# Moving the overflow branch behind the seventh quad's first products, the routing weights ahead, and the scaled residual off TensorE, in a two-layer decoder kernel

## The chip, the cores and the metric

The kernel runs on one core of a Trainium2 chip. The metric is the device time of one execution in microseconds: the median of the runs shown. All tensors are float32.

## What is computed

256 tokens of width 1024 pass two layers. Each has a mixer (layer 0: a gated MLP beside latent attention; layer 1: sparse attention in three branches), and behind it a mixture of 32 experts in 4 groups of 8. Each sub-layer ends in `x <- LN(alpha*x + f(x))`:

```python
for layer in range(DEPTH):
    ...
    x = layer_norm(DN_ALPHA * x + mix, ln1_g[layer], ln1_b[layer])
    ffn = hier_moe(x, ...)
    x = layer_norm(DN_ALPHA * x + ffn, ln2_g[layer], ln2_b[layer])
```

`hier_moe` picks one group per token by softmax, then two of its eight experts, and sums `silu(x w_gate) * (x w_up) * weight` times `w_down` over the chosen experts. The weights of all experts are 96 MB per layer; all are read.

## The kernel before, in words

**Weights.** Every weight matrix comes from memory as a piece of 1 MB into one of 23 places in SBUF (`Ring`, L106 to L140). `ring.free` gives a place back and at once records the load of the next piece in it, on SyncE's queue (SP). SP issues in order. At most eight loads are under way: each takes the semaphore of the eighth before it, so in a busy stretch SP issues one when one has landed.

**End of a mixer.** `project` (L448) forms `alpha*x + y w_o` in four PSUM banks `acc[t][h]` (token half t, column half h). The first matmul on each is `aident` (the identity times alpha) by `x`; then come eight steps of three matmuls each on operands that were split in a high and a low part by ScalarE (ACT) and VectorE (DVE). `close_mixer` (L476) copies the sums to `x` by ACT and takes their moments by DVE (`raw`, L481), transposes them, forms the router's logits, and picks groups and experts on DVE (`route`, L1227; `rank`, L1268; `places`, L1352, a 0/1 matrix of slots by tokens). Idle stretches of TensorE (PE) are filled with matmuls that nobody reads (`warm`, L335).

**Experts.** The 32 experts are taken as eight quads (`QUADS` gives the order); a quad works on 128 slots, 32 tokens for each of its four experts, or on two such chunks for quads 6 and 7 of layer 1 (`STATIC_CHUNKS`). A quad has twelve pieces: eight for gate and up (`gate_up`, L1417), four for down (`down`, L1454). `quad(i)` (L1490) forms the gate and up products of its tokens, gathers the tokens of the next quad (`pick`, L1367), prepares the way back (`back`, L1390), turns the hidden values, multiplies by down, and leaves the scatter into the sums `acc` for the next quad's gate and up products (`flush`). In the first quad three things are still missing and are recorded behind its gate and up products: the routing weights (`weights0`, `weights1` in `rest`, L549), `back` of the first quad, and `alpha*x` in the sums (four `aident` matmuls, L1524).

**Overflow.** Should an expert have over 32 tokens (64 in a quad of two chunks), `overflow` (L1292) does the rest in loops under a branch (`tc.If`, L1299) that every engine takes: each loads a count into a register, compares, and jumps over the body when it is zero. It stands between quads 5 and 6 (`OVERFLOW_AT = 6`, L1567 to L1575). With these inputs the body isn't entered.

The order of instructions on an engine is the order in which the code records them inside `manual_schedule`; the mixers and the first steps of `project` (`AUTO`) are ordered by a scheduler.

Of the kernel before, what the change touches and what calls it, by code (L numbers as in the profile page):

```python
# [142 lines left out]
def trunk(ctx, tc, a, out):  # L143
# [109 lines left out]
    aident = consts.tile([128, 128], F32, name="aident")  # L253
    idb = consts.tile([128, 128], BF16, name="idb")
    zerob = consts.tile([128, 128], BF16, name="zerob")
# [11 lines left out]
    def more_constants():  # L267
# [4 lines left out]
        V.memset(zerob, 0.0)  # L272
        V.tensor_scalar(aident, ident, ALPHA, None, op0=ALU.mult)
# [174 lines left out]
    def project(l):  # L448
# [27 lines left out]
    def close_mixer(l, rb, acc, step, products):  # L476
# [50 lines left out]
        for h in range(2):  # L527
            mm(acc2[0][h], zerob, idb[:, None, :].to_broadcast([128, 4, 128]), True, False)
        warm(2)
# [5 lines left out]
        for h in range(2):  # L535
            mm(acc2[1][h], zerob, idb[:, None, :].to_broadcast([128, 4, 128]), True, False)
        warm(W1[0])
# [16 lines left out]
        return rt, acc2, (xg, [second] + affines, rest)  # L554
# [737 lines left out]
    def overflow(l, rt, acc):  # L1292
# [6 lines left out]
        with tc.If(value(8, 56) > 0):  # L1299
# [7 lines left out]
    def more(l, q, g, acc):  # L1307
# [8 lines left out]
        p = ps("C")  # L1316
# [73 lines left out]
    def back(q, rt, dd, tr, often=True):  # L1390

        d, dw = dd[:, 0:256], (p2() if dd.shape[1] == 256 else dd[:, 256:512])[:, 0:256]
        V.tensor_tensor(dw.rearrange("p (t e s) -> p t e s", t=2, e=4), d.rearrange("p (t e s) -> p t e s", t=2, e=4),
                        rt[1][:, :, 4 * q:4 * q + 4, None].to_broadcast([128, 2, 4, 32]), op=ALU.mult)
        p = ps(tr)
# [13 lines left out]
    def gather(q, rt, base, tr):  # L1409
# [5 lines left out]
        return xg, *back(q, rt, dd, tr, often)  # L1415

    def gate_up(l, q, xgs, between):  # L1417

        hp = [ps("CO"[i]) for i in range(len(xgs))]
        for k in range(KC):  # L1420
# [6 lines left out]
            ring.free((l, q, k))  # L1427
# [50 lines left out]
    def moe_layer(l, rt, acc, begun):  # L1478
# [3 lines left out]
        gs, late = [(begun[0], None, None)], begun[1:]  # L1482
# [7 lines left out]
        def quad(i):  # L1490
# [4 lines left out]

            def between(k):
# [196 lines left out]
```

## Time and profile before

| | |
|---|---|
| median of 3 runs | 700.41 us (700.06 to 701.95) |
| the profiled execution's own time | 700.38 us |
| its span, first to last instruction | 698.7 us |
| PE busy | 619.1 us, 89% |
| DVE busy | 284.3 us, 41% |
| ACT busy | 204.5 us, 29% |
| DMA, mean over the span | 337 GB/s |
| mean granted clock of PE | 0.956 of full speed |

The span is cut in stretches, and for each the profile tells how long every engine was busy, which share of its full clock PE was granted, and how busy the 16 DMA engines were. In a stretch with PE idle the row of what it waited for says why. A stretch with PE never idle is limited by PE's own work, one with the DMA engines at a share of 1 is moving weights as fast as it can, and both can hold at once.

### The profile page before, as it was taken

Reading aid. Unit: us, or ns where it says so; the run is one execution under the profiler, and the core shown is the slowest. Engines: PE = TensorE matmul, PEld = TensorE weight load, DVE = VectorE, ACT = ScalarE, POOL = GpSimd, SP = SyncE. Lnnn points to the kernel's source line nnn. Section 1 sums busy time; section 2 is a strip of 40 time slices with the busy share of each in tenths; the row PEclk is TensorE's granted clock in tenths of the full one; section 3 lists DMA queues with packets and bytes.
Section 4 is the critical chain, followed back from the end, with each engine's and each line's share of the span. In section 5 each row is a group of like instructions: output and inputs, shape, how many; then the busy total and the mean of one; then the engine's idle time right before and its main releaser. Section 6 shows DMA issues by size and latency. Waiting matters only on the chain. (4 is left out here: it accounts for less than half of the span.)

```text
span 698.7 us, 11137 instructions
## 1 busy us (share of the span) xinstructions
PE 619.1 (89%) x4459; PEld 386.7 (55%) x4459; DVE 284.3 (41%) x709; ACT 204.5 (29%) x514; POOL 49.6 (7%) x56
## 2 busy tenths in 40 slices
PE   7799999799999685887999999999799899897883
PEld 5678676464555141423988776685554554644331
DVE  4757736522222120206848897444422212312116
ACT  5554534121111010103546676431111111202011
POOL 4611000000000000002420000000000000000002
PEclk9999999989999988997999999999899999999797
DMA  8946879949999999999498450399689999999961
GB/s 344 418 184 247 334 264 380 398 189 425 419 420 418 423 420 416 421 420 416 161 422 342 127 235 1 129 394 401 280 353 420 420 422 421 420 419 422 414 266 60
DMA packets 34068, 235.62 MB, mean 337 GB/s; under 512 B 3920, under 2 KB 4688, under 8 KB 6224
## 3 DMA queue, kind: packets, MB, share of 16 engines
q1 hardware_dynamic: 34000, 234.75, 82.7%
q8 instruction: 38, 0.62, 0.4%
q14 instruction: 30, 0.25, 0.1%
HBM read 233.69 MB, written 1.05 MB: 336 GB/s over the span
## 5 line engine op out<-in xcount | busy, mean ns | idle before, releaser
L182 PE MATMUL psC<-ring,w 128*32 128x512 f32 (+1 forms) x1040 | 132.5, 618 | 24.5 <-PEq L1299 13.1
L182 PEld LDWEIGHTS psC<-ring,w 128*32 128x32 f32 (+1 forms) x1040 | 31.2, 114 | 90.0 <-issue 48.5
L182 PE MATMUL psA<-ring,ring 128*128 128x256 f32 (+1 forms) x480 | 80.1, 315 | 0.0
L182 PE MATMUL psT<-ring,p 128*32 128x512 f32 (+1 forms) x608 | 68.8, 587 | 3.1 <-DMA ring<-in_moe 2.2
L182 PEld LDWEIGHTS psA<-ring,ring 128*128 128x128 f32 x480 | 67.5, 193 | 6.5 <-issue 1.8
L182 PEld LDWEIGHTS psT<-p,x 128*128 128x128 f32 x512 | 64.5, 208 | 10.9 <-issue 10.1
L182 PE MATMUL psT<-p,x 128*128 128x128 f32 x512 | 67.3, 295 | 0.0
L1437 DVE SCALAR_TENSOR_TENSOR p<-p,psC 128x256 f32<-128x256 f32 x16 | 6.7, 421 | 133.5 <-ACT p L1436 133.3
L317 DVE TENSOR_TENSOR p<-psT,p 128x256 fp32r<-128x256 f32 x72 | 30.5, 424 | 62.8 <-ACT p L316 62.8
L1436 ACT ACTIVATE p<-psC 128x256 f32<-128x256 f32 x16 | 6.1, 383 | 170.2 <-PE psC L182 170.2
L316 ACT ACTIVATE p<-psT 128x256 fp32r<-128x256 f32 x72 | 27.5, 383 | 63.2 <-PE psT L182 42.2
L290 POOL TENSOR_TENSOR sm<-sm,mhalf 128x1 f32<-128x1 f32 (+1 forms) x12 | 7.7, 647 | 511.4 <-DVE sm L287 280.6
L182 PEld LDWEIGHTS psA<-p,k 128*128 128x128 f32 x144 | 25.2, 192 | 30.1 <-issue 17.6
L182 PE MATMUL psA<-p,k 128*128 128x256 f32 x144 | 39.4, 313 | 1.6 <-DVE sm L1560 1.6
L312 DVE TENSOR_TENSOR ring<-ring,ring 128x1024 fp32r<-128x1024 f32 (+1 forms) x28 | 36.0, 1301 | 8.0 <-ACT ring L311 7.7
L182 PEld LDWEIGHTS psT<-ring,p 128*32 128x32 f32 x608 | 17.3, 111 | 37.6 <-issue 25.3
L182 PE MATMUL psS<-ring,ring 128*128 128x416 f32 (+3 forms) x128 | 32.0, 384 | 2.0 <-ACT ring L311 1.5
L182 PE MATMUL psO<-ring,ring 128*64 128x256 f32 (+3 forms) x248 | 32.2, 349 | 1.1 <-DVE ring L333 0.7
L311 ACT ACTIVATE ring<-ring 128x1024 fp32r<-128x1024 f32 (+1 forms) x32 | 31.8, 1031 | 3.6 <-issue 1.3
L182 PE MATMUL psS<-p,k 128*128 128x256 f32 x144 | 29.9, 288 | 0.0
L1377 DVE COPY w<-psT 128x512 f32<-128x512 f32 x16 | 11.1, 691 | 44.2 <-PE psT L182 44.2
L1111 ACT ACTIVATE ring<-psS,sm 128x128 f32<-128x128 f32 (+1 forms) x64 | 26.2, 420 | 7.8 <-DVE sm L1102 7.7
(282 smaller groups left out, 844.4 us busy)
## 6 DMA issues: line engine op xcount, KB each, us to landing
ring<-in_moe SPq DMA_DIRECT2D x192, 1024.0 KB, 19.5
ring<-in_m SPq DMA_DIRECT2D x23, 1024.0 KB, 10.0
ring<-in_vec SPq DMA_DIRECT2D x2, 1024.0 KB, 18.1
ring<-in_m SPq DMA_DIRECT2D x2, 832.0 KB, 6.0
x<-in_x SPq DMA_DIRECT2D x2, 512.0 KB, 5.2
out<-x SPq DMA_DIRECT2D x4, 256.0 KB, 2.0
ring<-in_m SPq DMA_DIRECT2D x1, 768.0 KB, 15.0
ring<-in_m SPq DMA_DIRECT2D x1, 736.0 KB, 18.9
```

The costliest lines, as they stand in the source:

```text
L182: T.matmul(o, lhsT, rhs, start=start, stop=stop, skip_group_check=True)
L290: G.tensor_tensor(r, t, mhalf[:, :n], op=ALU.pow)
L311: S.activation(hi, src, AF.Copy)
L312: (sub or V).tensor_tensor(lo, src, hi.bitcast(F32), op=ALU.subtract)
L316: S.activation(hi, src, AF.Copy)
L317: V.tensor_tensor(lo, src, hi.bitcast(F32), op=ALU.subtract)
L1111: S.activation(p[:, i * w:(i + 1) * w], sx[c, u][:, i * w:(i + 1) * w], AF.Exp, bias=nb[:, i0 + i:i0 + i + 1], accum_out=su[:, i0 + i:i0 + ...
L1377: (S.activation(dst, p[0], AF.Copy) if f == 0 else V.tensor_copy(dst, p[0]))
L1436: S.activation(e, p[:, 0:256], AF.Tanh, scale=0.5)
L1437: V.scalar_tensor_tensor(e, e, 1.0, p[:, 0:256], op0=ALU.add, op1=ALU.mult)
```

## The change

- The overflow branch moves from in front of quad 6 to behind that quad's gate and up products. `quad` becomes a generator that stops there (`yield`). The eight places of these products are given back, and the slots of the next quad formed, only behind the branch. PE gets a branch hint, recorded just before those products, with the label of the branch. In the body the bank "C" gives way to "O".
- The routing weights (`weights0`, `weights1`, and the weighted one-hot matrix of the first quad, now `weighted`) are recorded behind the first of the eight gate and up steps of the first quad. For the other quads `weighted` is recorded together with `places`, ahead of `back`.
- `alpha*x` gets into the experts' sums by four ACT instructions that write PSUM (`residual`), in place of four `aident` matmuls. In `project` the four `aident` matmuls go as well: `raw` forms `alpha*x + acc` by one DVE instruction per half, and takes the moments from the result in SBUF.
- The zero matmuls that opened the sums become matmuls of `warm`, in the same number. `router_prep(1)` moves from quad 3 to quad 5 of layer 0. The scratch space for DMA descriptors grows from 512 to 1024 bytes per partition.

```diff
         def products(t, i):
             k = ks[i]
-            if i == 0:
-                for h in range(2):
-                    mm(acc[t][h], aident, x[:, t, HALF[h]], True, False)
...
-                mm3(acc[t][h], y, w, False, i == KC - 1)
+                mm3(acc[t][h], y, w, i == 0, i == KC - 1)
...
         def raw(t):
 
             for h in range(2):
-                S.activation(x[:, t, HALF[h]], acc[t][h], AF.Copy)
-            return x[:, t], *stats(acc[t])
+                V.scalar_tensor_tensor(x[:, t, HALF[h]], x[:, t, HALF[h]], ALPHA, acc[t][h], op0=ALU.mult, op1=ALU.add)
+            return x[:, t], *stats([x[:, t, HALF[h]] for h in range(2)])
...
-        def rest():
+        def shares():
             weights0()
             weights1()
-            return (xg, *back(0, rt, dd, "O"))
+            return weighted(0, rt, dd, p2()[:, 0:256])
...
-        with tc.If(value(8, 56) > 0):
+        with tc.If(value(8, 56) > 0, label=f"beyond{l}"):
...
+            def residual(h):
+                for t in range(2):
+                    S.activation(acc[t][h], x[:, t, HALF[h]], AF.Copy, scale=ALPHA)
...
             def between(k):
                 nonlocal rb
+                if i == 0 and k == 1:
+                    late[1] = late[1]()
                 if i == 0 and k >= KC // 2:
                     late[0].pop(0)()
                     if k == KC - 1:
                         late[0].pop(0)()
+                        residual(0)
                 if k in (2, 4):
                     flush(2)
-                if k == 4:
-                    dds.append(places(nq, rt, 0.0))
-                if k == 5 and i == 3 and l == 0:
+                if k == 4 and i != OVERFLOW_AT:
+                    onehots(0)
+                if k == 5 and i == 5 and l == 0:
                     rb = router_prep(1, "T")
 
-            hp = gate_up(l, q, [g[0] for g in gs], between)
+            later = [] if i == OVERFLOW_AT else None
+            hp = gate_up(l, q, [g[0] for g in gs], between, later)
+            if i == OVERFLOW_AT:
+                yield
+                ring.free(*later)
+                onehots(0)
...
-                    if i == 0:
-                        for t in range(2):
-                            for h in range(2):
-                                mm(acc[t][h], aident, x[:, t, HALF[h]], False, False)
...
+            if i == 0:
+                residual(1)
...
         for i in range(OVERFLOW_AT):
-            quad(i)
-        flush(len(pending))
+            drain(quad(i))
         yield
+        tc.no_sync_barrier()
+        tc.mark_branch_hint_location(f"beyond{l}", hint="LikelyTaken", engines=[mybir.EngineType.PE])
+        broken = quad(OVERFLOW_AT)
+        with tc.manual_schedule():
+            next(broken)
         overflow(l, rt, acc)
         tc.no_sync_barrier()
         with tc.manual_schedule():
-            for i in range(OVERFLOW_AT, NQ - 1):
-                quad(i)
+            drain(broken)
+            for i in range(OVERFLOW_AT + 1, NQ - 1):
+                drain(quad(i))
             mr = last_quad()
```

What the code doesn't tell at once is where this puts instructions on an engine. PE at the end of the first quad's gate and up products in layer 0 (`psO` the transposed one-hots and, by `oneh`, the sums of weights; `psT<-p,x` the gathering of the next quad; `ring` a weight place), before:

```order
L182 MATMUL psC_1136<-ring_699,w_152_1121 32x512 x4
L1397 MATMUL psO_1251<-ident,k_149_1112 128x128 x2
L182 MATMUL psO_1251<-oneh,p_163_1249 128x1 x2
L182 MATMUL psT_1265<-p_158_1175,x 128x128 x8
L182 MATMUL psT_1275<-p_158_1175,x 128x128 x8
L1449 MATMUL psC_1285<-ident,p_167_1260 128x128 x2
L182 MATMUL psA_1033<-x,aident 128x512
L182 MATMUL psA_1034<-x,aident 128x512
L182 MATMUL psS_1035<-x,aident 128x512
L182 MATMUL psS_1036<-x,aident 128x512
L1397 MATMUL psO_1294<-ident,p_158_1175 128x128 x2
L182 MATMUL psT_1303<-ring_701,p_167_1260 32x512 x4
```

and with the change:

```order
L182 MATMUL psC_1128<-ring_695,w_152_1113 32x512 x4
L1389 MATMUL psO_1246<-ident,k_149_1104 128x128 x2
L182 MATMUL psO_1246<-oneh,p_156_1155 128x1 x2
L182 MATMUL psT_1260<-p_159_1189,x 128x128 x8
L182 MATMUL psT_1270<-p_159_1189,x 128x128 x8
L1444 MATMUL psC_1280<-ident,p_167_1255 128x128 x2
L1389 MATMUL psO_1284<-ident,p_159_1189 128x128 x2
L182 MATMUL psO_1284<-oneh,p_159_1189 128x1 x2
L182 MATMUL psT_1295<-ring_697,p_167_1255 32x512 x4
```

On PE only the four `aident` rows are gone; what moved is on DVE, whose order at the same quad before was this (L1383 brings the gathered tokens out of PSUM, first half and second half; L493 applies gain and bias to `x`; L1254 to L1264 are the weights of one token half, L1393 the weighted one-hots):

```order
L1383 TENSOR_SCALAR w_152_1121<-psT_1123,col 128x128 x2
L1383 TENSOR_SCALAR w_152_1121<-psT_1162,col 128x128 x2
L1358 TENSOR_TENSOR p_158_1175<-rk_1103,cst 128x256
L493 TENSOR_TENSOR x<-x,psT_1183 128x512 x2
L493 TENSOR_TENSOR x<-x,psT_1196 128x512 x2
L493 TENSOR_TENSOR x<-x,psT_1209 128x512 x2
L493 TENSOR_TENSOR x<-x,psT_1216 128x512 x2
L1254 TENSOR_SCALAR rt_1056<-rt_1056 128x1
L1256 TENSOR_TENSOR rt_1056<-rt_1056 128x1
...
L1264 SCALAR_TENSOR_TENSOR w_121_1017<-rt_1093 128x32
L1393 TENSOR_TENSOR p_163_1249<-k_149_1112,w_121_1017 128x256
L1403 COPY wsl_1258<-psO_1251 128x1
```

and is now:

```order
L1372 TENSOR_SCALAR w_152_1113<-psT_1115,col 128x128 x2
L1243 TENSOR_SCALAR rt_1048<-rt_1048 128x1
L1245 TENSOR_TENSOR rt_1048<-rt_1048 128x1
...
L1253 SCALAR_TENSOR_TENSOR w_121_1009<-rt_1085 128x32
L1381 TENSOR_TENSOR p_156_1155<-k_149_1104,w_121_1009 128x256
L1372 TENSOR_SCALAR w_152_1113<-psT_1176,col 128x128 x2
L1347 TENSOR_TENSOR p_159_1189<-rk_1095,cst 128x256
L1381 TENSOR_TENSOR p_159_1189<-p_159_1189,w_121_1009 128x256
L486 TENSOR_TENSOR x<-x,psT_1198 128x512 x2
L486 TENSOR_TENSOR x<-x,psT_1211 128x512 x2
```

The weights now stand between the two halves of the gathered tokens, that is, in front of an instruction that PE's fifth gate and up step needs. Third, PE at the overflow branch of layer 0, before (`psA`, `psS` the scatter into the sums, then the branch; the gate and up products of quad 6 follow behind the skipped body):

```order
L182 MATMUL psS_1036<-p_263_2070,k_240_1887 128x256 x2
L182 MATMUL psA_1034<-p_263_2070,k_240_1887 128x256
L1296 TENSOR_LOAD ct_1104
L1299 COMPARE_AND_BRANCH
...
L1299 UNCONDITIONAL_BRANCH
L182 MATMUL psC_4070<-ring_1796,w_251_2000 32x512 x4
L182 MATMUL psC_4070<-ring_1810,w_251_2000 32x512 x4
```

and with the change:

```order
L1703 BRANCH_PREFETCH_HINT
L182 MATMUL psC_2070<-ring_1778,w_251_1993 32x512 x4
L182 MATMUL psC_2070<-ring_1792,w_251_1993 32x512 x4
L182 MATMUL psA_1025<-p_259_2040,k_237_1869 128x256
...
L182 MATMUL psC_2070<-ring_1833,w_251_1993 32x512 x4
L182 MATMUL psC_2070<-ring_1878,w_251_1993 32x512 x4
L1285 TENSOR_LOAD ct_1096
L1288 COMPARE_AND_BRANCH
...
L1288 UNCONDITIONAL_BRANCH
L182 MATMUL psT_4121<-p_802_4113,x 128x128 x8
```

All eight gate and up steps and the four scatters stand between the hint and the branch now, and the gathering of the last quad's tokens is the first thing behind it. SP's and GpSimd's rows are the same in both kernels, with the branch behind the same load.

## Rows read from the trace of the kernel before

**Rows 1.** Busy time, granted clock and DMA share of chosen stretches (us from the start).

```profile
core 0 of [0], span 698.7 us
core 0: us, PE busy (x) PEld busy (x) DVE busy (x) ACT busy (x) POOL busy (x), PEclk, DMA share, GB/s
95.00:111.40 16.40, 16.40 (x86) 13.73 (x85) 5.37 (x11) 5.12 (x8) 0.54 (x1) 1.00 0.85 317
134.90:139.20 4.30, 0.08 (x2) 0.04 (x1) 3.00 (x18) 0.96 (x6) 0.00 (x0) 1.00 1.02 429
139.20:146.50 7.30, 7.30 (x36) 7.30 (x37) 1.06 (x3) 1.25 (x3) 0.00 (x0) 0.53 0.67 278
147.00:152.00 5.00, 5.00 (x26) 2.33 (x28) 0.92 (x3) 0.72 (x2) 0.00 (x0) 1.00 0.00 0
230.00:320.00 90.00, 67.19 (x458) 28.10 (x458) 11.20 (x27) 8.86 (x22) 0.00 (x0) 0.89 1.01 420
446.00:462.00 16.00, 16.00 (x76) 12.90 (x75) 5.27 (x9) 4.82 (x8) 0.00 (x0) 1.00 0.88 350
503.00:508.00 5.00, 5.00 (x26) 2.33 (x28) 0.80 (x3) 0.60 (x2) 0.00 (x0) 1.00 0.00 0
510.00:640.00 130.00, 124.58 (x1065) 65.34 (x1058) 29.42 (x71) 22.66 (x55) 0.00 (x0) 1.00 1.01 421
642.50:649.00 6.50, 0.00 (x0) 0.00 (x0) 0.23 (x1) 0.00 (x0) 0.00 (x0) 0.65 1.01 411
649.00:655.00 6.00, 5.96 (x32) 1.75 (x36) 0.20 (x1) 0.00 (x0) 0.00 (x0) 0.52 1.01 415
```

**Rows 2.** Timeline of PE behind the first gate and up products, layer 0.

```profile
139.16 0.92 PE L182 MATMUL psO<-oneh,p 128*128 128x1 f32 x4 [4.22 <-DVE p L1393]
139.95 6.76 PE L182 MATMUL psT<-p,x 128*128 128x128 f32 x32
146.76 1.88 PE L182 MATMUL psA<-x,aident 128*128 128x512 f32 x4
...
150.19 0.38 PE L1397 MATMUL psO<-ident,p 128*128 128x128 f32 x2
```

**Rows 3.** The matmuls by `aident` into psA (two records each; psS has as many).

```profile
L182 PE MATMUL psA<-x,aident x16: 592/592/697, 79.0 to 503.9; 128*128 128x512 f32 x16
```

**Rows 4.** Single lines: copies to x, moments, and a DVE operation on PSUM (min/median/max ns).

```profile
L484 ACT ACTIVATE x<-psS x4: 597/598/599, 110.9 to 468.1; 128x512 f32<-128x512 f32 x4
...
L413 DVE BATCH_NORM_STATS2 sm<-psS x4: 698/698/699, 111.5 to 468.8; 128x6 f32<-128x512 f32 x4
...
L562 DVE SCALAR_TENSOR_TENSOR x<-psA,sm,ring x4: 742/743/747, 325.0 to 689.6; 128x512 f32<-128x512 f32 x4
```

**Rows 5.** What PE waited for from 508 to 690 us (total, times, longest).

```profile
PE psC L182 <- PEq L1299: 6.6, 1, 6.6
PE psO L182 <- DVE p L1393: 6.1, 8, 1.0
```

**Rows 6.** The overflow branch, by engine, one in each layer (min/median/max ns).

```profile
L1299 DVEq COMPARE_BRANCH  x2: 63/68/72, 262.0 to 641.7; - x2
L1299 PEldq COMPARE_BRANCH  x2: 5988/6180/6372, 262.4 to 642.2; - x2
```

**Rows 7.** Two loads of expert weights: issue, and time to landing.

```profile
L124 SPq DMA_DIRECT2D ring<-in_moe x1: 328/328/328, 152.0 to 152.0; - x1
...
DMA to landing us min/median/max: 5.1/5.1/5.1
...
L124 SPq DMA_DIRECT2D ring<-in_moe x1: 339/339/339, 658.4 to 658.4; - x1
...
DMA to landing us min/median/max: 16.3/16.3/16.3
```

**Rows 8.** Timeline at the end of layer 1: last down product, first row of the closing norm.

```profile
684.15 1.07 PE L182 MATMUL psT<-ring,p 128*32 128x256 f32 x16
...
688.92 0.74 DVE L562 SCALAR_TENSOR_TENSOR x<-psA,sm,ring 128x512 f32<-128x512 f32 x1
```

More of the change, by code (lines that the diff above doesn't have):

```diff
@@ L526, in close_mixer @@
         acc2 = [[ps("A"), ps("A")], [ps("S"), ps("S")]]
-        for h in range(2):
-            mm(acc2[0][h], zerob, idb[:, None, :].to_broadcast([128, 4, 128]), True, False)
-        warm(2)
+        warm(4)
         xt = transposed(nn[1][0], True)
@@ L534, in close_mixer @@
         o1 = logits(l, xt)
-        for h in range(2):
-            mm(acc2[1][h], zerob, idb[:, None, :].to_broadcast([128, 4, 128]), True, False)
-        warm(W1[0])
+        warm(W1[0] + 2)
         weights1 = route(scaled(1, o1), 1, selb, w32)
@@ L1388, in pick, with weighted, back @@
         return lambda: half(1)
-    def back(q, rt, dd, tr, often=True):
-        d, dw = dd[:, 0:256], (p2() if dd.shape[1] == 256 else dd[:, 256:512])[:, 0:256]
+    def weighted(q, rt, d, dw):
         V.tensor_tensor(dw.rearrange("p (t e s) -> p t e s", t=2, e=4), d.rearrange("p (t e s) -> p t e s", t=2, e=4),
                         rt[1][:, :, 4 * q:4 * q + 4, None].to_broadcast([128, 2, 4, 32]), op=ALU.mult)
+        return dw
+    def back(d, dw, tr, often=True):
         p = ps(tr)
@@ L1414, in gather, with gate_up @@
         pick(dd, xg)()
-        return xg, *back(q, rt, dd, tr, often)
-    def gate_up(l, q, xgs, between):
+        return xg, *back(dd[:, 0:256], weighted(q, rt, dd[:, 0:256], dd[:, 256:512]), tr, often)
+    def gate_up(l, q, xgs, between, later=None):
         hp = [ps("CO"[i]) for i in range(len(xgs))]
@@ L1426, in gate_up @@
                        slot[:, j * 512:(j + 1) * 512], k == 0, k == KC - 1)
-            ring.free((l, q, k))
+            if later is None:
+                ring.free((l, q, k))
+            else:
+                later.append((l, q, k))
         return hp
@@ L1481, in moe_layer @@
         order = QUADS[l]
-        gs, late = [(begun[0], None, None)], begun[1:]
+        gs, late = [(begun[0], None, None)], list(begun[1:])
         pending = []
@@ L1494, in quad, with onehots @@
             dds = []
+            def residual(h):
+                for t in range(2):
+                    S.activation(acc[t][h], x[:, t, HALF[h]], AF.Copy, scale=ALPHA)
+            def onehots(c):
+                dd = places(nq, rt, -32.0 * c)
+                dds.append((dd[:, 0:256], weighted(nq, rt, dd[:, 0:256], dd[:, 256:512])))
             def between(k):
                 nonlocal rb
+                if i == 0 and k == 1:
+                    late[1] = late[1]()
                 if i == 0 and k >= KC // 2:
@@ L1515, in quad @@
                 xg = halves_of(w4())
-                pick(dds[c], xg)()
+                pick(dds[c][0], xg)()
                 if c + 1 < nn:
-                    dds.append(places(nq, rt, -32.0 * (c + 1)))
+                    onehots(c + 1)
                 if c == 0:
                     hts = turn_hidden(hs)
-                    if i == 0:
-                        for t in range(2):
-                            for h in range(2):
-                                mm(acc[t][h], aident, x[:, t, HALF[h]], False, False)
-                ngs.append((xg, *back(nq, rt, dds[c], "O")))
+                ngs.append((xg, *back(*dds[c], "O")))
+            if i == 0:
+                residual(1)
             for c0, slots in ((0, (8, 9)), (512, (10, 11))):
```

12 lines of the change are left out of this document (4 added, 8 removed).

## The prediction, made before the changed kernel ran

> **What bounds the kernel now.** I read the stretches first, then the waits of TensorE (PE), then the loads. Three regimes alternate. (a) PE alone: at the end of each mixer it is never idle, 16.40 of 16.40 us in layer 0 and 16.00 of 16.00 in layer 1, with the DMA engines below their full share [rows 1]; what PE does there counts in full. (b) Loads alone: from 230 to 320 us, the second half of layer 0's experts, the DMA engines are full (1.01, 420 GB/s) while PE works 67 of 90 us [rows 1]. What PE saves there is lost; only an earlier start of the stream helps. (c) Both: from 510 to 640 us, layer 1's experts, the DMA engines are full and PE is busy 124.6 of 130 us [rows 1]. PE is the one behind there: layer 1's last weight load lands at 658.4 + 16.3 = 674.7 us [rows 7] and its product starts at 684.2 [rows 8]. So the loads have a margin of 9.5 us at the end, and a kernel that saves more than that on PE alone meets the loads.
>
> The loads start late for PE's sake: in each layer the DMA engines stand wholly still for 5.0 us, 147 to 152 and 503 to 508 [rows 1], since all places are full and the next is given back only by the first quad's down products. The first load behind the pause takes 5.1 us [rows 7] where the full stream gives 1.05 MB / 420 GB/s = 2.5 us, so a pause costs the stream 5.0 + 2.6 = 7.6 us. From then on it runs full to the last piece. Two quantities have to be followed therefore, PE's time and the stream's.
>
> **Part by part, per layer unless said.**
>
> *`aident` matmuls.* 32 records, two to a matmul [rows 3]: four in `project` and four in the first quad of each layer. The four of the quad take 150.19 − 146.76 = 3.4 us [rows 2]. Those are gone in full: their place is taken by four ACT instructions of about 0.6 us [rows 4], at a time when ACT waits for PE; without that cover they would cost 2.4. Those of `project` cost the same 3.4 and PE is full there, but the high and low parts of the next operands have to be ready that much sooner. Bounds 0 and 3.4; I take 3.0, as ACT and DVE are busy only 5.1 and 5.4 of 16.4 us there [rows 1].
>
> *`raw`.* Before, ACT copies (0.60) and DVE's moments (0.70 per half) follow it, about 0.6 + 1.4 = 2.0 us to the moments; now DVE does both in turn, 2 x 0.74 + 2 x 0.70 = 2.9 [rows 4]. PE's transposes wait for two DVE instructions instead of two of ACT, 0.3 more. For the second token half the moments are on the path to the routing: cost 0.9 us, I take 1.0 (bounds 0.3 and 2.9). Net of the two: PE reaches the first gate and up products 2.0 us earlier.
>
> *Weights made early.* PE waits 4.22 us for DVE before the `oneh` matmuls [rows 2], and the pause brings its granted clock to 0.53, the 1.2 GHz level, for the 7.3 us of the next gathering [rows 1]: at most 7.3 x 0.47 = 3.4 us, of which I take 2.7, as not all in that stretch goes with the clock. The work itself (3.0 us busy on DVE over a chain of 4.2 [rows 1]) now runs beside the gate and up products. It stands in DVE's order ahead of the second half of the gathered tokens, which PE needs at its fifth step; four steps of gate and up and the second gathering lie between, about 5 us, so I cost it at nothing, with under 1 us to spare. Together with the four `aident`: 4.2 + 2.7 + 3.4 = 10.3 us earlier at the first down product.
>
> *The stream.* The first down product comes 2.0 + 10.3 = 12.3 us earlier, more than the 7.6 us of the pause, so the pause closes; the pieces before it come 2.0 us earlier. Shift of the stream: 9.6 us in each layer.
>
> *`weighted` ahead of `back`.* In layer 1 PE waits for this DVE operation eight times, 6.1 us in all [rows 5]; it now stands at the fifth step of the products before. Gain up to 6.1 on PE. In layer 0 the loads hide it.
>
> *The branch.* On PE it takes 6.0 and 6.4 us [rows 6], 6.6 of waiting in layer 1 [rows 5], and again a clock of 0.52 for the next 6.0 us [rows 1]: 6.0 x 0.48 = 2.9. In layer 0 it lies in regime (b) and costs nothing. Moved, DVE and ACT take theirs while PE still multiplies. On PE the price behind a hint isn't in this trace: the lower bound is a branch as DVE executes it, 0.07 us [rows 6], the upper the 6.4 it takes now, plus the clock. I take 0.5: the hint stands some 10 us ahead, longer than 6.4. Gain 9.0 in layer 1, bounds 0 and 9.5. Behind the branch stand eight places to be given back. SP is behind PE there anyway: the last expert piece goes out at 658.4 [rows 7], over 9 us after PE began the products that free its place (end of the pause at 649.0 [rows 1]); nothing is lost.
>
> The Trainium skill says in "Runtime: NRT & Kernel Launch", section "Instruction fetch mechanics", that an engine fetches its instructions purely in sequence and that a taken branch out of the loaded window waits for a fetch. The 6.4 us of PE agree with the second half; by the first a hint could do nothing. That is the first rival below.
>
> *Rest.* The zero matmuls become as many of `warm`; `router_prep` lies in regime (b); the scratch space serves a queue that moves nothing here. Nothing for each.
>
> **Sum.** Layer 0 ends with its loads: −9.6 us, and all of layer 1 starts that much earlier. PE in layer 1: −9.6 − 2.0 − 10.3 − 6.1 − 9.0 = −37.0. The stream: −9.6 − 9.6 = −19.2, so the last piece lands at 655.5, where PE would want it at 684.2 − 37.0 = 647.2. The loads decide: 655.5 − 684.2 = −28.7. As PE now waits for pieces in the last quad, I add back 1.2 us for work at the lower clock: the tail from there to the norm is 4.8 us [rows 8], about half of it PE's. So −27.5: 700.4 − 27.5 = **672.9**, say 673 us. The sum is made against the profiled execution's 700.38, which is the median within 0.03.
>
> **Rivals.**
> 1. *The hint does nothing* (the page's rule). PE keeps 6.6 us at the branch, now with the gathering and the turn of the last quad at the low clock behind it: −37.0 + 9.0 = −28.0 for PE, against −28.7 for the loads. Both end within a microsecond; with waits of both kinds in turn I add 1.5: 674.5. For it: the trace shows no hinted branch executed. Against: nothing in the trace. Because the loads decide either way, the branch is worth little.
> 2. *The later routing costs the clock.* The pause between the last `warm` and the first gathering grows by 1 us. If that brings PE to 1.2 GHz at the start of gate and up, a window as long as those seen (6 us at 0.52 [rows 1]) costs 2.9 more in each layer: the stream shifts 9.6 − 2.9 = 6.7 per layer, 13.4 in all, and the end −(13.4 + 9.5) + 1.2 = −21.7: 679. For it: the clock fell behind the pause of 4.2 us and that of 6.5 [rows 1]; against: this one grows by 1 us alone.
> 3. *DVE is late with the second half.* If the chain of weights is not over in the 5 us, PE waits up to 4.2 us at the fifth step and falls to the low clock (2.7): of the 10.3 us 3.4 remain. The stream then moves 2.0 + 3.4 = 5.4 per layer, 10.8; end −(10.8 + 9.5) + 1.2 = −19: 681.
> 4. *Slower.* The matmuls by `aident` were the cover of the splits. Without them, and with `raw` on DVE, PE waits for every split: 0.60 on ACT and 0.70 on DVE a half [rows 4], 16 halves, 20.8 us per layer. Taken in full in both layers, 41.6 − 27.5 = +14: 714. It decides from two thirds of the halves on. Against: ACT and DVE are idle two thirds of that stretch, and PE never [rows 1].
>
> **How the numbers follow.** Forecast 58%, rival 1 25%, rival 2 9%, rival 3 5%, rival 4 3%. Upward the range takes in rivals 1 to 3 and a `project` that gives nothing besides. Downward: with 3.4 for `project`, 0.3 for `raw` and a stream that follows PE in full, the shift is 7.6 + 3.1 = 10.7 per layer, and if PE's whole 12 to 13 us pass to the stream, 12.5: the end −(25.0 + 9.5) = −34.5, 666. I give 664 to 684. A difference under 0.3% (2 us) couldn't be told from none. Only rival 4 ends slower (3%), some 2% lie within 0.3% where half of it happens; faster 95%.
>
> **What would show it.** Right: no PE wait for L1393's successor behind the first gate and up products, and the clock at 1.00 there; no stretch of DMA share 0 around the first down products; eight waits fewer in layer 1; PE waiting for `ring<-in_moe` in the last quad of layer 1, where it waits for none now; the last piece landing near 655 us and PE's branch under 1 us. Wrong: the last product of layer 1 still several us behind its piece (then PE decides, and one of its terms fell short), or a pause of the DMA engines that is still there; a PE idle in `project` would point to rival 4.

## The result, and the profile after

The changed kernel takes 670.38 us (median of 4 runs, 669.59 to 670.56), against 700.41: the ratio is 0.9565, with a 95% interval of 0.9548 to 0.9582. The forecast was 673.0, with a range of 664 to 684. The profiled execution took 670.22 us, its span is 668.5.

First the chain that ended last, from the page of the changed kernel, by line:

```profile
DMA ring<-in_moe 39%; PE psA L182 11%; PE psT L182 9%; PE psC L182 8%; PE psS L182 8%; PE psO L182 5%; DMA ring<-in_m 3%; PE psT L1122 1%; PE psT L1123 1%; DVE x L560 1%; PE psT L1124 1%; ACT ring L1100 0%; DVE x L477 0%; DVE sm L409 0%; DVE sm L765 0%
```

The way to the end now runs through loads of expert weights for 39% of the span. (In the kernel before, the chain can be followed back for the last 50 us only, and no load stands in them.) Next, milestones on PE's timeline. Of the kernel before: a row of the first mixer that the change doesn't touch, the first gate and up products and the first down products of layer 0, then both of layer 1.

```profile
72.92 1.05 PE L182 MATMUL psC<-ring,w 128*128 128x128 f32 x8
...
120.81 3.64 PE L182 MATMUL psC<-ring,w 128*32 128x512 f32 x32
...
150.85 3.64 PE L182 MATMUL psT<-ring,p 128*32 128x512 f32 x32
...
477.41 3.64 PE L182 MATMUL psC<-ring,w 128*32 128x512 f32 x32
...
506.73 3.64 PE L182 MATMUL psT<-ring,p 128*32 128x512 f32 x32
```

The same of the changed kernel, with the rows around the first gathering behind those products, which answer to [rows 2], and the last down product, which answers to [rows 8]:

```profile
71.36 1.05 PE L182 MATMUL psC<-ring,w 128*128 128x128 f32 x8
...
117.11 3.64 PE L182 MATMUL psC<-ring,w 128*32 128x512 f32 x32
...
131.08 0.50 PE L182 MATMUL psO<-oneh,p 128*128 128x1 f32 x4
131.44 3.82 PE L182 MATMUL psT<-p,x 128*128 128x128 f32 x32
...
135.97 2.35 PE L182 MATMUL psT<-ring,p 128*32 128x512 f32 x20
...
464.60 3.89 PE L182 MATMUL psC<-ring,w 128*32 128x512 f32 x32
...
483.70 3.64 PE L182 MATMUL psT<-ring,p 128*32 128x512 f32 x32
...
654.02 1.07 PE L182 MATMUL psT<-ring,p 128*32 128x256 f32 x16
```

The `oneh` matmuls have no wait ahead of them any more, and the gathering takes 3.82 us where it took 6.76. The untouched row in the first mixer starts 1.56 us earlier. I take that for no work of the change: across the twelve kernels of the experiments the row lies between 70.32 and 73.80, and between 70.32 and 73.40 in the ten whose program is the changed kernel's up to there. With one trace of each kernel this can't be shown, though, and the medians differ by 30.0 us, as much as the traces do with the start left in. With the 1.56 taken off, the milestones compare with the forecast so:

| | before | after | difference | less 1.56 | forecast |
|---|---|---|---|---|---|
| first gate and up products, layer 0 | 120.81 | 117.11 | −3.70 | −2.1 | −2.0 |
| first down product, layer 0 | 150.85 | 135.97 | −14.88 | −13.3 | −12.3 |
| first gate and up products, layer 1 | 477.41 | 464.60 | −12.81 | −11.3 | −11.6 |
| first down product, layer 1 | 506.73 | 483.70 | −23.03 | −21.5 | −21.9 |
| last weight piece lands | 674.7 | 652.8 | −21.9 | −20.3 | −19.2 |
| last down product | 684.15 | 654.02 | −30.13 | −28.6 | −28.7 |
| time | 700.38 | 670.22 | −30.16 | −28.6 | −27.5 |

Busy time, granted clock and DMA share by stretch, changed kernel: the first gathering and the first down products of layer 0 (where the pause was), layer 1's routing, its branch, its last quad (columns as in [rows 1]).

```profile
131.00:136.00 5.00, 5.00 (x50) 4.99 (x50) 2.26 (x5) 1.64 (x4) 0.00 (x0) 1.00 1.02 428
136.00:156.00 20.00, 20.00 (x177) 10.13 (x180) 4.48 (x12) 5.06 (x12) 0.00 (x0) 1.00 1.01 420
456.00:464.60 8.60, 6.88 (x44) 5.43 (x43) 5.02 (x28) 2.32 (x4) 0.38 (x1) 0.83 1.02 423
620.00:630.00 10.00, 7.83 (x76) 5.34 (x68) 2.58 (x6) 1.75 (x4) 0.00 (x0) 1.00 1.01 415
642.00:653.00 11.00, 8.00 (x43) 1.95 (x44) 1.67 (x4) 1.54 (x4) 0.00 (x0) 0.53 0.96 398
```

Against [rows 1]: the clock is 1.00 behind the first gate and up products (0.53 before), the DMA engines are full through the first down products (share 0 for 5.0 us before), and the stretch behind the branch keeps its clock (0.52 before). New are a clock of 0.83 in layer 1's routing and 0.53 in the last quad.

What PE waited for from 490 to 665 us, which answers to [rows 5]; the branch, to [rows 6]; the last piece, to [rows 7]:

```profile
PE psC L182 <- DMA ring<-in_moe: 2.3, 2, 1.3
```

```profile
L1288 DVEq EVENT_SEMAPHORE  x4: 21/21/21, 253.1 to 618.6; - x4
...
L1288 DVEq COMPARE_BRANCH  x2: 63/68/72, 247.5 to 612.9; - x2
L1288 PEldq COMPARE_BRANCH  x2: 482/1444/2407, 265.7 to 619.0; - x2
```

```profile
L124 SPq DMA_DIRECT2D ring<-in_moe x1: 339/339/339, 636.6 to 636.6; - x1
...
DMA to landing us min/median/max: 16.2/16.2/16.2
```

Both the 6.6 us behind the branch and the eight waits for the weighted one-hots are gone. PE now waits for loads instead, 2.3 us in the last quad. Its branch takes 0.48 us in layer 0 and 2.41 in layer 1, where it took 5.99 and 6.37.

### The profile page after: what moved, and what is told of

Read it like the earlier page. It is cut to its first block, busy times and chain, and to the rows that moved or that the text cites. A ratio compares the mean times of both kernels' runs of the same rounds, so it can differ in the third digit from the quotient of the medians.

```text
span 668.5 us, 11058 instructions
## 1 busy us (share of the span) xinstructions
PE 603.0 (90%) x4427; PEld 374.9 (56%) x4427; DVE 290.4 (43%) x715; ACT 204.6 (31%) x514; POOL 48.3 (7%) x56
## 4 chain that ended last, share of the span: by engine, by line
PE 45%; DMA 41%; DVE 5%; ACT 2%; issue 1%; DVEq 0%; SPq 0%; ACTq 0%
DMA ring<-in_moe 39%; PE psA L182 11%; PE psT L182 9%; PE psC L182 8%; PE psS L182 8%; PE psO L182 5%; DMA ring<-in_m 3%; PE psT L1122 1%; PE psT L1123 1%; DVE x L560 1%; PE psT L1124 1%; ACT ring L1100 0%; DVE x L477 0%; DVE sm L409 0%; DVE sm L765 0%
## 5 line engine op out<-in xcount | busy, mean ns | idle before, releaser
L182 PE MATMUL psC<-ring,w 128*32 128x512 f32 (+1 forms) x1040 | 134.4, 617 | 20.6 <-DMA ring<-in_moe 20.6
L182 PEld LDWEIGHTS psC<-ring,w 128*32 128x32 f32 (+1 forms) x1040 | 29.2, 112 | 84.9 <-issue 40.4
L182 PEld LDWEIGHTS psT<-p,x 128*128 128x128 f32 x512 | 59.8, 195 | 13.9 <-issue 8.8
L182 PE MATMUL psT<-p,x 128*128 128x128 f32 x512 | 62.8, 282 | 3.7 <-DVE p L1347 1.5
```

Source lines behind the costliest of these rows:

```text
L182: T.matmul(o, lhsT, rhs, start=start, stop=stop, skip_group_check=True)
```

## Experiments

All edits are against the changed kernel, whose ratio is 0.9565 (0.9548 to 0.9582). Times are medians, each ratio is against the kernel before on the same chip (its median was 700.1 to 700.5 us on each), with its 95% interval. Where a trace is compared with the changed kernel's "from the untouched row", each start is taken off as above.

| kernel | us | ratio (interval) |
|---|---|---|
| no hint | 669.71 | 0.9560 (0.9539 to 0.9580) |
| branch at its old place, no hint | 672.15 | 0.9610 (0.9582 to 0.9639) |
| two pieces fewer | 664.90 | 0.9503 (0.9479 to 0.9527) |
| two pieces fewer, no hint | 670.36 | 0.9567 (0.9539 to 0.9595) |
| weights late | 684.80 | 0.9774 (0.9748 to 0.9799) |
| alpha x by PE in the first quad | 674.28 | 0.9623 (0.9599 to 0.9647) |
| alpha x by PE in `project` | 674.11 | 0.9627 (0.9606 to 0.9647) |
| weighted one-hots late | 671.63 | 0.9586 (0.9565 to 0.9607) |
| warm in layer 1's routing | 669.86 | 0.9561 (0.9548 to 0.9574) |
| warm in layer 1's last quad | 671.17 | 0.9574 (0.9561 to 0.9587) |
| both | 670.82 | 0.9571 (0.9557 to 0.9584) |
| hint a quad earlier | 670.64 | 0.9579 (0.9556 to 0.9602) |

### What bounds the end, and what the hint is worth

Four kernels ran on one chip. The first takes the hint away:

```diff
-        tc.mark_branch_hint_location(f"beyond{l}", hint="LikelyTaken", engines=[mybir.EngineType.PE])
```

> The changed kernel with the hint for TensorE (PE) taken out; the branch stays behind the seventh quad's gate and up products. Theory A (the loads decide at the end of layer 1): PE's branch takes 6 us again and the gathering behind it runs at the low clock, but PE waits less for its last pieces instead, and the last piece lands where it did: +1.0 to +2.0 us, about 672. Rival B (PE decides, the branch is worth its time): +6 to +9 us, 677 to 679. Rival C (the hint does nothing, and something else shortened PE's branch): PE's branch stays at 0.5 and 2.4 us and the time at 670.4.

Measured 669.71: no difference from the changed kernel, where theory A had 1 to 2 us. The hint does act on PE, though. PE's branch, and its timeline in layer 1 (last gate and up products ahead of the branch, gathering and turn behind it), without the hint, and the DVE row that the gathering waits for:

```profile
L1288 PEldq COMPARE_BRANCH  x2: 6039/6068/6096, 266.5 to 620.2; - x2
```

```profile
618.84 3.64 PE L182 MATMUL psC<-ring,w 128*32 128x512 f32 x32
626.95 5.32 PE L182 MATMUL psT<-p,x 128*128 128x128 f32 x32 [4.46 <-DVE p L1347]
632.10 0.38 PE L1444 MATMUL psC<-ident,p 128*128 128x128 f32 x2
```

```profile
626.47 0.42 DVE L1347 TENSOR_TENSOR p<-rk,cst 128x256 f32<-128x256 f32 x1 [12.38 <-PEq L1288]
```

and with the hint:

```profile
617.69 3.64 PE L182 MATMUL psC<-ring,w 128*32 128x512 f32 x32
622.11 3.73 PE L182 MATMUL psT<-p,x 128*128 128x128 f32 x31 [0.77 <-DVE p L1347]
627.23 0.27 PE L182 MATMUL psT<-p,x 128*128 128x128 f32 x1 [1.39 <-issue]
627.34 0.38 PE L1444 MATMUL psC<-ident,p 128*128 128x128 f32 x2
```

From the start of the last products to the turn 13.26 us without the hint and 9.65 with it: 3.6 us on PE, which the time doesn't show. The wait for DVE is the branch's all the same, since DVE in turn waits for PE's branch. The branch's own 6.1 us shrink to a wait of 4.46, as its record starts 2.3 us before the products end, and from its end to the gathering 0.7 more pass.

Where the 3.6 us go can be read in the last quad. With the hint PE waits 2.3 us for gate and up pieces there, its clock falls to 0.53, and its last down product starts 1.24 us behind the landing of its piece (654.02 against 652.78). Without the hint PE has no wait for gate and up pieces, the clock stays at 1.00, and the product starts 0.13 us behind its piece (654.67 against 654.54):

```profile
642.00:653.00 11.00, 7.46 (x71) 2.13 (x69) 1.75 (x4) 1.53 (x4) 0.00 (x0) 1.00 0.99 412
```

So PE's time at the branch is off the path, unless something else hid it. The test of that takes two loads out of the stream:

```diff
+FEWER = (1, 1), (1, 6)
...
+            if (l, q) in FEWER and i % 12 == 7:
+                continue
...
-            slot = ring.get((l, q, k))
+            once = (l, q) in FEWER
+            slot = ring.get((l, q, 6 if once and k == 7 else k))
...
-                ring.free((l, q, k))
+                if not (once and k == 6):
+                    ring.free((l, q, 6 if once and k == 7 else k))
```

> The changed kernel with two of layer 1's weight pieces not loaded (the eighth gate and up piece of its third and fourth quad; the seventh is multiplied twice in its place, so PE's work is the same and that part of the result is another). Two pieces are 2.5 us of the full stream each. Theory A (the loads decide at the end): the last piece lands 5.0 us earlier, PE follows until it is the bound itself, and no longer waits in the last quad: 3 to 5 us faster, 665.5 to 667.5. Rival B (PE decides): no change, 670.4.

Measured 664.90, 5.5 us less, a little over the 3 to 5 of theory A. From the untouched row the last piece lands 4.6 us earlier, and PE, at a clock of 1.00 from 637 to 648 us, stays close behind it. PE doesn't wait for a load in the last quad any more, and its last down product comes at 648.47, 0.1 us behind its piece (632.2 + 16.1 = 648.3). So the loads did decide, and with two pieces fewer both engines are level. Then the hint must count:

> Both edits together: two pieces fewer and no hint. With the loads out of the way the branch's time on PE must show: Theory A: 4 to 8 us slower than the kernel with two pieces fewer alone, and so near the changed kernel without the hint or 2 us under it. Rival C (the hint does nothing): the same as two pieces fewer alone.

Measured 670.36: 5.5 us more than with the hint, where the same edit cost nothing with all loads in place. In the traces the last down product is 5.5 us later (653.99 against 648.47), of which 1.4 lie in the start (72.97 against 71.54 at the untouched row) and 3.8 between the last products ahead of the branch and the turn (13.26 against 9.50). With the start taken off, the hint is worth 4.1 us here.

> The changed kernel with the branch back ahead of the seventh quad, all groups of the sixth added first, without a hint. Theory A (the loads decide): PE pays 6.4 us of branch and up to 3 us of low clock ahead of the seventh quad, but more pieces are still to be landed behind it: +1 to +3 us. Rival B (PE decides): +9 us, 679. If this comes out as the kernel without the hint at the new place, the place by itself is worth nothing.

The edit puts the loop of the quads back round the branch and drops the hint. Measured 672.15, 1.8 us more (2.5 in the traces from the untouched row); the intervals meet at their ends, so that there is a loss is likely, and its size isn't resolved. PE pays what it paid before the change, 6.5 us of waiting and the low clock behind it:

```profile
PE psC L182 <- PEq L1288: 6.5, 1, 6.5
```

```profile
621.00:627.00 6.00, 5.69 (x28) 1.58 (x32) 0.85 (x2) 0.00 (x0) 0.00 (x0) 0.50 1.01 415
```

So place and hint together are worth some 2 us of the 30, by the intervals at most some 5.5, as long as the loads decide.

### The first quad: weights and residuals

```diff
-                if i == 0 and k == 1:
-                    late[1] = late[1]()
...
-                gs = [late[2](late[1])]
+                gs = [late[2](late[1]())]
...
```

The next quad's `weighted`, which needs the weights, moves behind them too.

> The changed kernel with the routing weights and the first two quads' weighted one-hots made behind the first quad's gate and up products again. Theory A (the early weights close the pause of the DMA engines): PE waits 4 us for DVE and runs 7 us at the low clock behind it in each layer, the first down product comes about 7 us later, and the stream loses 4.7 to 7 us in each layer: +9 to +14 us, 679 to 684. Rival (the four matmuls less and the other parts close the pause alone, and PE's wait is hidden in both layers): under +4 us.

Measured 684.80, 14.4 us more, at the upper end of theory A: the largest single part. In this trace PE waits 4.2 us for the weighted one-hots (L1381) in layer 0 again, the clock falls (0.57 from 135 to 140 us), and the pause is back in both layers:

```profile
PE psO L182 <- DVE p L1381: 4.9, 2, 4.2
```

```profile
140.00:145.00 5.00, 4.32 (x28) 4.08 (x27) 1.02 (x2) 0.98 (x2) 0.00 (x0) 0.74 0.27 110
145.00:150.00 5.00, 5.00 (x50) 1.58 (x50) 1.43 (x4) 2.82 (x7) 0.00 (x0) 1.00 0.53 182
495.00:500.00 5.00, 4.32 (x28) 4.08 (x27) 1.02 (x2) 0.98 (x2) 0.00 (x0) 0.74 0.14 57
500.00:505.00 5.00, 5.00 (x51) 1.65 (x50) 1.43 (x4) 2.75 (x7) 0.00 (x0) 1.00 0.52 172
```

The missing DMA share is (0.73 + 0.47) x 5 = 6.0 us in layer 0 and (0.86 + 0.48) x 5 = 6.7 in layer 1: 12.7 of the 14.4 us are the stream's.

The residual sums by PE (the ACT copies go, their place in the program is that of the kernel before; here and in the next experiment the constant `aident` comes back, and the scratch space for DMA descriptors goes back to 512 bytes):

```diff
+                    if i == 0:
+                        for t in range(2):
+                            for h in range(2):
+                                mm(acc[t][h], aident, x[:, t, HALF[h]], True, False)
```

> The changed kernel with alpha x added to the first quad's sums by four matmuls with the scaled identity again instead of four ACT copies; the first down product comes 3.4 us later in each layer. Theory of the forecast (the pause closes with some us to spare, so the stream doesn't move): 0 to +1 us. Rival (the stream follows PE's first down product one for one, since the places are given back later by as much): +3.4 us in each layer, +6.8 in all, 677.

Measured 674.28, 3.9 us more, between the two (2.4 in the traces from the untouched row): some half of PE's 6.8 us reach the end. The stretches show why:

```profile
140.00:145.00 5.00, 5.00 (x42) 2.12 (x44) 0.58 (x2) 1.05 (x3) 0.00 (x0) 1.00 0.67 231
488.00:493.00 5.00, 5.00 (x35) 2.17 (x38) 0.16 (x1) 0.77 (x2) 0.00 (x0) 1.00 0.72 267
493.00:498.00 5.00, 5.00 (x48) 2.01 (x44) 2.55 (x6) 1.15 (x3) 0.00 (x0) 1.00 0.93 367
```

A short pause opens again in each layer, 0.33 x 5 = 1.65 us and (0.28 + 0.07) x 5 = 1.75 us, 3.4 together. So of the 3.4 us per layer some 1.7 were to spare, and the rest was needed to keep the stream full.

### The projection

```diff
+            if i == 0:
+                for h in range(2):
+                    mm(acc[t][h], aident, x[:, t, HALF[h]], True, False)
...
-                V.scalar_tensor_tensor(x[:, t, HALF[h]], x[:, t, HALF[h]], ALPHA, acc[t][h], op0=ALU.mult, op1=ALU.add)
-            return x[:, t], *stats([x[:, t, HALF[h]] for h in range(2)])
+                S.activation(x[:, t, HALF[h]], acc[t][h], AF.Copy)
+            return x[:, t], *stats(acc[t])
```

> The changed kernel with the four matmuls with the scaled identity in each projection and the copies by ACT behind it, as before. Theory of the forecast (net 2.0 us on PE a layer): +4.0 us, 674.4. Rival, as the trace read (3.7 us at the first gate and up products of layer 0): +7.4 us, 677.8, less some 2 us if the window at half the clock in layer 1's routing goes with it.

Measured 674.11, 3.7 us more, near the forecast's 4.0. The traces split it otherwise. From the untouched row PE's first gate and up products come 2.1 us later in layer 0, and those of layer 1 only 1.0 us more, 3.1 in all; the end comes 1.9 later. In layer 1 the window of low clock is gone with the edit (granted clock 1.00 from 455 to 472 us, 0.83 in the changed kernel's routing), as the last clause of the rival had it. So in layer 1 the clock seems to take back about half of the 2 us. The larger figure of the rival was the 3.70 of the table above with the 1.56 of the start still in it.

### The later weighted one-hots

```diff
-                dds.append((dd[:, 0:256], weighted(nq, rt, dd[:, 0:256], dd[:, 256:512])))
+                dds.append((dd[:, 0:256], dd[:, 256:512]))
...
+                weighted(nq, rt, *dds[c])
```

> The changed kernel with each later quad's weighted one-hots made just ahead of the products that use them. Theory A (the loads decide): PE waits about 6 us more in layer 1, in eight pieces, and less for its last pieces: 0 to +2 us. Rival B (PE decides): +6 us, 676.5.

Measured 671.63, 1.2 us more, with overlapping intervals; the traces from the untouched row have 3.3. The waits are there, 6.7 us of them from 490 to 665 us, and at most half of them show in the time:

```profile
PE psO L182 <- DVE p L1381: 5.4, 7, 1.0
...
PE psC L1444 <- DVE p L1381: 1.3, 1, 1.3
```

### Clock windows, and a hint given earlier

The first two fill waits for DVE in layer 1's routing and waits for loads in its last quad, with matmuls whose result nobody reads:

```diff
-        warm(W1[0] + 2)
+        warm(W1[0] + (2, 4)[l])
...
-        warm(W1[1])
+        warm((W1[1], 3)[l])
```

> The changed kernel with 2 more matmuls that keep PE busy ahead of layer 1's ranks and 3 more ahead of its first gathering, all of them in time in which PE waits for DVE (0.85 and 0.87 us). Theory (the window at half the clock at 461.7 us delays layer 1's first gate and up products, its stream and so the end): the window is gone, 1.3 to 2 us faster, 668.4 to 669. Rival (the clock falls there whatever stands in those waits, or PE is late by the added matmuls): 0 to +0.5 us.

Measured 669.86: not to be told from the changed kernel. The edit did its part. PE's first gathering of layer 1, in the changed kernel and then with the edit:

```profile
461.31 3.36 PE L182 MATMUL psT<-k,x 128*128 128x128 f32 x16 [0.87 <-DVE sm L1272]
```

```profile
462.56 2.02 PE L182 MATMUL psT<-k,x 128*128 128x128 f32 x16 [0.21 <-DVE sm L1272]
464.51 3.64 PE L182 MATMUL psC<-ring,w 128*32 128x512 f32 x32
```

The gathering is 1.3 us shorter, but starts later: from the untouched row of each to the first gate and up products 392.6 us (464.51 − 71.94) against 393.2 (464.60 − 71.36). That leaves 0.7 us on PE, less than the runs resolve.

```diff
-                warm(WARM[l], "O")
+                warm(WARM[l] if l == 0 else 4 * (k in (6, 7)), "O")
```

> The changed kernel with 4 matmuls that keep PE busy ahead of each of the last two gate and up pieces of layer 1's last quad, where PE waits 0.98 and 1.29 us for the pieces. Theory (the 10.2 us at half the clock from 642.6 us on cost PE 2.6 us at the down products, of which 1.2 count, since the last piece lands 1.2 us ahead of its use): 0.5 to 1.2 us faster. Rival (the wait for DVE behind it lowers the clock all the same, or the pieces are late anyway): 0 to +0.5 us.

Measured 671.17: no gain, and by its interval no loss of more than 2 us. Where PE waited 2.3 us for gate and up pieces it now waits 0.5 us for a down piece, and the clock falls all the same, a little later:

```profile
652.45 1.94 PE L182 MATMUL psT<-ring,p 128*32 128x256 f32 x16 [0.54 <-DMA ring<-in_moe]
```

These last 16 products take 1.94 us where they took 1.07. Ahead of them PE still waits for the chain of the hidden values, 1.6 us for DVE and 0.5 for ACT, which no added matmul covers.

> Both of the edits together. If both are right and add up: 1.8 to 3.2 us faster, 667.2 to 668.6. If only the first counts, since the stream still decides at the end: 1.3 to 2 us faster.

Measured 670.82: the two don't add up to anything. No version that loads all pieces beats the changed kernel by more than its interval.

The last run moves the hint ahead of the sixth quad:

```diff
         for i in range(OVERFLOW_AT):
+            if i == OVERFLOW_AT - 1:
+                tc.no_sync_barrier()
+                tc.mark_branch_hint_location(f"beyond{l}", hint="LikelyTaken", engines=[mybir.EngineType.PE])
             drain(quad(i))
         yield
         tc.no_sync_barrier()
-        tc.mark_branch_hint_location(f"beyond{l}", hint="LikelyTaken", engines=[mybir.EngineType.PE])
```

> The changed kernel with the hint one quad earlier, some 22 us more ahead of the branch in layer 1, which came 9 us behind its hint there and took PE 2.4 us, and 21 us behind it in layer 0, where it took 0.48. Theory (the 2.4 us are the rest of a fetch that is not yet done): PE's branch takes about 0.5 us in both layers, and the time stays within 1 us of 670.4, since the loads decide. Rival (the fetched code is lost again when the hint is given too early, or the 2.4 us are something else): 2.4 or 6 us in layer 1.

Measured 670.64, and the theory is wrong; of the rival, "something else" is left. Hint and branch of this kernel, and the branch of the kernel with alpha x by PE in `project`, whose hint stands 9 us ahead:

```profile
L1705 PEldq BRANCH_PREFETCH_HINT  x2: 36/40/45, 215.5 to 579.3; - x2
...
L1288 PEldq COMPARE_BRANCH  x2: 483/1475/2467, 266.0 to 620.3; - x2
...
L1293 PEldq COMPARE_BRANCH  x2: 477/802/1127, 269.1 to 623.1; - x2
```

41 us ahead in layer 1 the branch takes 2.47 us, 9 us ahead it took 2.41; in layer 0 it is 0.48 both times. So the 2.4 us are not the rest of a fetch that was begun too late. Nor are they a fixed price: with the hint 9 us ahead the record takes between 1.13 and 2.43 us in layer 1, depending on the kernel. They cost PE little, since the record lies beside the last products: in the changed kernel these run from 617.69 to 621.33, the branch from 619.02 to 621.43. What the time in the record is stays open.

The stop that PE makes behind the branch without a releaser moves as well. In the changed kernel it ends before the last matmul of the gathering, 5.80 us after the branch (627.23 against 621.43); with alpha x by PE in `project` before the 15th, 5.65 us after it (629.91 against 624.26):

```profile
629.91 2.27 PE L182 MATMUL psT<-p,x 128*128 128x128 f32 x18 [1.94 <-issue]
```

## Why the prediction was right

**The end is set by the loads, and PE meets them.** This carried the forecast: PE was to gain 37.0 us in all, the stream 19.2, and 28.7 were to reach the last down product. It came 28.6 earlier, once the start is set aside, PE waits for `ring<-in_moe` in the last quad, and two pieces fewer give 5.5 us. That the loads decide is shown. That 28.6 meets 28.7 so closely is luck: from the untouched row the last piece landed 20.3 us earlier where 19.2 were forecast, and PE started its last down product 1.24 us behind the piece where the forecast had it at once. PE's own sum was too high as well. With two pieces fewer, where PE waits for no load from 484 us on, its last down product comes 34.3 us earlier than before (684.15 − 648.47, less 1.38 of start), not 37.0. So PE led the stream by less than the 8.3 us of the forecast.

**`aident` in `project` and `raw`.** Net 2.0 us a layer forecast; 2.1 on the timeline of layer 0, and 2.1 again when undone. Shown for layer 0. In layer 1 undoing it gives 1.0, the low clock of the routing going with it.

**Weights early.** 4.2 of waiting and 2.7 of clock forecast, with the residuals 10.3; the first down product of layer 0 gained 13.3 − 2.1 = 11.2. The gathering gave 6.76 − 3.82 = 2.94 of it, the wait 4.22, the matmuls 3.4, which leaves 0.6 to smaller things. DVE was in time with the second half of the gathered tokens (no such wait in either layer), so rival 3 did not happen.

**The stream.** This is the term that was mis-sized. The forecast set the whole advance of the first down product, 12.3 us, against a pause of 7.6 and found some to spare, so that the stream would move by 9.6 a layer whether or not PE kept the residual matmuls. But the pieces ahead of the pause move with the first 2.0 us; only the 10.3 (measured 11.2) count against the pause. And the pause costs more than 7.6: with the residuals back on PE, 11.2 − 3.4 = 7.8 us of advance, 1.7 us of it were open again. The landings give its price. In layer 0 the third last piece to land ahead of the pause lands 4.3 us earlier than before, the last piece of the layer 13.3 (issue and time to landing, before and then after):

```profile
L124 SPq DMA_DIRECT2D ring<-in_moe x1: 337/337/337, 302.9 to 302.9; - x1
...
DMA to landing us min/median/max: 15.9/15.9/15.9
...
L124 SPq DMA_DIRECT2D ring<-in_moe x1: 337/337/337, 289.3 to 289.3; - x1
...
DMA to landing us min/median/max: 16.2/16.2/16.2
```

So the closed pause was worth 9.0 us; in layer 1, with 12.9 ahead of it and 21.9 at the last piece, it was 9.0 again. The forecast counted the 5.0 us of standstill and the first load behind them; in the trace the last piece ahead of the pause and the third behind it were late as well, by 1.3 and 1.0 us against the 2.5 from piece to piece of the full stream. The stream moved by 13.3 − 1.56 = 11.8 us in layer 0, not 9.6.

That the first gate and up products of layer 1 still came out near the forecast (−11.3 against −11.6) is again two misses that cancel. PE's first row of layer 1 was 14.65 us earlier (327.10 to 312.45), but 2.3 of that were lost in the next 18 us, where the clock was 0.57 for 7 us (312.4 to 319.4; 0.76 in the same place before, 327 to 334) and DVE late with `x` by 1.2 us. And the mixer of layer 1 gave some 0.5 us, not 2.0, for the low clock of its routing.

**`weighted` ahead of `back`.** Up to 6.1 us on PE in layer 1; undone, PE waits 6.7 us and the time grows by 1.2, which the intervals don't tell from nothing (3.3 in the traces). Right, and worth little, as the loads decide.

**The branch.** 9.0 us on PE were forecast, with 0.5 left, and a branch under 1 us was named as a sign of being right; in layer 1 its record took 2.41, though beside the products. Left on PE are 0.77 of waiting for DVE behind it and 1.39 without a releaser, 2.2 us. At the old place it costs 6.5 us and some 3.0 of clock (6 us at 0.50), so 7.3 are gained. The low end of the bounds, 0.07 us "as DVE executes it", was misread: the compare itself takes 0.07 us there, but DVE's last record of that line in layer 1 comes at 618.6, 5.6 us behind the compare at 612.9. DVE too stands for the branch, only beside PE's products. That the time wouldn't show the branch was forecast, and shown: no hint, no difference.

**The rivals.** Rival 1, a hint that does nothing, is refuted: 0.48 and 2.41 us with it, 6.04 and 6.10 without. The Trainium skill's page "Runtime: NRT & Kernel Launch", section "Instruction fetch mechanics", has the fetch purely in sequence, from which the prediction concluded that a hint could do nothing; here the measurement differs from that. The time of rival 1 was off as well: without a hint the kernel took 669.71 us, not 674.5, and nothing of the 1.2 and 1.5 us that it adds back showed. Rival 2 happened in part: the clock fell in layer 1's routing, 0.83 over 8.6 us, and not in layer 0's. It cost the first gathering 1.3 us (3.36 against 2.02), where the rival had 2.9 in each layer, and with the `aident` matmuls back in `project` it was gone. Rival 4 did not happen: PE is busy 16.00 of 16.00 us from 90 to 106 us and 15.75 of 16.00 from 440 to 456, at the end of the two mixers.

**The rest of the difference.** Forecast 672.9, profiled 670.22: 2.7 us. 1.56 are the start of that execution, and 1.2 were added for the low clock behind the last down product. Those were not needed: from there to the end it is 14.5 us (668.5 − 654.02), as before (698.7 − 684.15 = 14.55). The clock did fall in the last quad (0.53), and PE began its last down product 1.24 us behind the piece; but that lies ahead of the product, and the earlier stream made up for it.

Undone one at a time, the parts cost 14.4 + 3.9 + 3.7 + 1.8 + 1.2 = 25.0 of the 30.0 us. What the rest is isn't shown: with two bounds so close the parts need not add up, and the `warm` matmuls in place of the zero matmuls and the place of `router_prep` were not undone.

## What to carry to other kernels

Where a stream of loads waits for places that one late product gives back, follow the stream and the engine as two sums: the same advance counts in full on the engine, on the stream only as far as the pause reaches, and only the part that the loads ahead of the pause don't share. Time an edit's worth against the other bound too: an edit that shows nothing (the hint) was worth 4 to 5.5 us as soon as two loads were gone. A forecast that comes out can hide misses that cancel, so check its milestones and not its end alone. Before two traces are subtracted, compare a row that the change can't touch.

## What the runs showed of the hardware

- Without a hint PE's record of the branch takes 5.9 to 6.4 us (four kernels, both layers). With one it takes 0.48 to 0.84 us in layer 0 and 1.13 to 2.47 in layer 1 (ten kernels), most of it beside the last products; the wait behind these is 0.69 to 0.84 us. How far ahead the hint stands, 9 or 41 us in layer 1, 21 or 50 in layer 0, made no difference. What sets the length of the record is open.
- Behind the hinted branch of layer 1 PE stands once more, for 0.4 to 1.9 us, and waits for nothing that the profile shows. Without the hint there is no such stop. Where it stands in the program differs from kernel to kernel, before the last matmul of the gathering in the changed kernel, before its 15th with alpha x by PE in `project`, but it ends 5.65 to 5.80 us after the branch's record in each of nine kernels; in the tenth, with the weighted one-hots late, a wait for DVE ends there. That is near the length of a branch without a hint. That the stop is a fetch too, begun at the branch, is a guess that wasn't tried.
- The compare of a branch is short on DVE (0.06 to 0.07 us), yet the engine's next records of the branch come some 5.6 us later in both layers (247.5 to 253.1, and 612.9 to 618.6).
- Up to a row that no edit changes, the start of the program differs by 3.5 us between profiled executions of nearly equal kernels (70.32 to 73.80), as much as some of the effects measured here. Nor is it a plain shift: where the row starts at 71.4 to 73.4, the first gate and up products follow it by the same 45.75 us within 0.02 in the kernels that are equal up to there; in the four that start at 70.3 to 70.7 they follow 0.8 to 1.1 us later.
